# One layer of a hybrid encoder trunk on one core: the value stage's transposed rows by VectorE for the second token half, token sums by token tile and one step later

## The chip, the cores and the metric

The kernel runs on one core of one Trainium2 chip. The core has TensorE (matmuls; PE in the profile, PEld its weight loads), VectorE (DVE), ScalarE (ACT), GpSimd (POOL) and SyncE (SP, whose queue issues nearly all DMAs here). The metric is the device time of one execution in microseconds; the figure compared is the median of several runs.

## The reference, cut to what matters

All inputs and outputs are f32; 2048 tokens of width 1024. The layer is a token mixer, a cross-attention into 256 memory tokens and a SwiGLU feed-forward, each with a norm before and after it:

```
y = concat([ya, yh]) @ w_out;           h = x + rms_norm(y, g_mix_post)
u = rms_norm(h, g_x_pre)
y = cross_attention(u, m, wq, wk, wv, wo);  h = h + rms_norm(y, g_x_post)
u = rms_norm(h, g_ffn_pre)
y = (silu(u @ w_gate) * (u @ w_up)) @ w_down
return h + rms_norm(y, g_ffn_post)
```

The change lies between the second and the third part: where `h` after the cross-attention is formed and `u` of the feed-forward is brought into the layout that the feed-forward's matmuls need.

## The kernel before, in words

f32 accuracy is kept by writing each operand as a high and a low part (`split2`: ScalarE rounds to the high part, VectorE subtracts to get the low part) and taking three products (`products`, lines 1162 to 1164).

The second half of the kernel is a row of jobs, and `phases` runs them: output projection (`mixed_block`), scores (`score_block`), values (`value_block`), the hidden layer for the first and the second half of the tokens (`hidden_blocks`), and the down projection in three pieces. A job is a 1024 x 1024 matrix (or part of one) that stays in SBUF as split tiles, the resident tiles `T`, against which blocks of 256 rows are streamed (`streamed`, tiles `S`). For the hidden layer the resident matrix is u, transposed: 1024 features by 1024 tokens of one half, and the weights are streamed. For the value job 16 token tiles of 128 rows are streamed in eight blocks; block n holds tiles n and n + 1.

A block is multiplied with seven products of quarters in place of eight (`seven`, a Strassen-like form, in the order 1, 5, 6, 3, 7, 2, 4); a product, one step, is 12 matmuls of 128x128 by 128x512. Steps 1, 2 and 3 use a quarter of the resident matrix as it is (`BLOCK`), steps 5, 7, 6 and 4 use sums and differences of quarters. Those are formed ahead by VectorE and kept in DRAM: for the weights by `combined`, for the second token half by `combined` too (`u_s`), for the first token half by `token_sums` (into `u0_s`; the profile leaves digits out of names and shows it as `u_s`). `resident` makes a T tile in two halves: a load into a row tile, then the split into `dst`. There are seven T slots; a slot comes free with its last use in the job before, so the hidden layer's tiles are split while the value job ends.

What a block does after its products is a generator (`after`), and each step moves every open generator on by one `yield`. `value_block.after` does, for its two row tiles: norm scale (line 1657), residual added (1661) and stored, mean squares, norm scale for the feed-forward (1670), then transposition. `transposed` does that with eight TensorE transposes of 128x128 (line 1423) into two PSUM banks and two ScalarE copies (1424); the result is stored into `u_d`. Blocks 4 and 6 (tokens 512 to 1023) then load back the transposed tile that lies 512 tokens earlier and form the sums (1461 to 1465).

`blocked` (line 1431) is another transposition, which the mixed and the score blocks use: VectorE transposes 32x32 blocks in two instructions of 128x512, and `store_blocked` stores the result in four DMAs, each from 32 partitions, such that what lies in DRAM has features on the partition axis.

The order in which each engine gets its instructions is set by a scheduler when the program is built: it goes by the order of the program and by when an instruction is ready in its own model of time. `issue_after` holds an instruction behind another; `behind` does that for a whole block of code, behind the last ScalarE and VectorE instruction of the present step. The splits of T tiles with a lag are put behind so.

Of the kernel before, what the change touches and what calls it, by code (L numbers as in the profile page):

```python
# [11 lines left out]
F32 = mybir.dt.float32  # L12
# [3 lines left out]
ALU = mybir.AluOpType  # L16
AX = mybir.AxisListType

P = 128
T = 2048  # L20
D = 1024
# [3 lines left out]
KT = D // P  # L25
NFF = DFF // P
NB = 2
TB = T // NB
NPB = TB // P
NT = T // P  # L30
# [18 lines left out]
class Layer:  # L49
# [111 lines left out]
    def run(self):  # L161
        tc, nc, I = self.tc, self.nc, self.I
        self._n = 0
        self.last = {}
        kw = dict(reuse_waits="tile")
        self.z_d = tc.dram_tile([DIN, T], F32, name="z_d")

        self.y_d = tc.dram_tile([NT, P, D], F32, name="y_d")
        self.un_d = tc.dram_tile([NPB, 2, P, 512], F32, name="un_d")
        self.h1t_d = tc.dram_tile([NT, 2, P, 512], F32, name="h1t_d")  # L170
        self.pt_d = tc.dram_tile([NT, 2, P, 512], F32, name="pt_d")
        self.h1_d = tc.dram_tile([T, D], F32, name="h1_d")
        self.h2_d = tc.dram_tile([T, D], F32, name="h2_d")
        self.qk_d = tc.dram_tile([D, D], F32, name="qk_d")
        self.vo_d = tc.dram_tile([D, D], F32, name="vo_d")
        self.u_d = tc.dram_tile([KT, P, T], F32, name="u_d")
        self.h_d = tc.dram_tile([NFF, P, T], F32, name="hid_d")
        self.y2_d = tc.dram_tile([T, D], F32, name="y2_d")
        with (
            tc.tile_pool(name="cst", bufs=1) as self.cst,  # L180
            tc.tile_pool(name="sm", bufs=3, **kw) as self.sm,
            tc.tile_pool(name="edge", bufs=1, side="right") as edge,
        ):
            self.consts()
# [281 lines left out]
    def in_first(self):  # L466
# [65 lines left out]
        def fetch():  # L532
            for s in range(2):
                for q in range(2):
# [11 lines left out]
                  for i, p in enumerate(self.ORDER)]  # L546
# [4 lines left out]
        phases = self.phases([(lambda i, j, a, n: raw[i, j][:, a:a + n, :], 4, blocks, None, {})], T)  # L551
# [451 lines left out]

    CHAIN = (5, 7, 6, 4)

    def resident(self, get, nk, key, dst, keep, sums):

        nc = self.nc  # L1010
        halves = [(0, (nk + 1) // 2), ((nk + 1) // 2, nk)]

        def fetched(a, b):
            if key in self.BLOCK:
                return get(*self.BLOCK[key], a, b - a), None
            if sums:
                return get(key, None, a, b - a), None
            if key == 5:
                return get(0, 1, a, b - a), get(0, 0, a, b - a)
            if key == 7:  # L1020
                return get(1, 1, a, b - a), get(0, 1, a, b - a)
            if key == 6:
                return keep[7][len(src)], get(0, 0, a, b - a)
            return get(1, 0, a, b - a), keep[6][len(src)]

        def split(a, b, t, o):
            if o is not None:
                nc.vector.tensor_tensor(t, t, o, ALU.add if key == 6 else ALU.subtract)
            self.split2(t, dst[:, 0, a:b], dst[:, 1, a:b], "A")

        src = []
        for a, b in halves:
            t, o = fetched(a, b)
            src.append(t)
            if key in (6, 7):
                keep[key] = src
            yield lambda a=a, b=b, t=t, o=o: split(a, b, t, o)
# [212 lines left out]
    def phases(self, jobs, first, prologue=None):  # L1250
# [51 lines left out]
        def half(g, tile):  # L1302

            if current[0] is None:
                if not queue:
                    return False
                free = min(slots, key=lambda s: s[1])
                if free[1] > g:
                    return False
                n, p, _ = k = queue.pop(0)  # L1310
                slots.remove(free)
                slots.append((free[0], uses[k][-1], free[2]))
                self._n += 1
# [5 lines left out]
                current[:] = [(k, self.resident(fetch(n, tile), jobs[n][1], p, dst, keep[n], jobs[n][3] is not None)), 0]  # L1319
# [51 lines left out]
        at = 0  # L1371
        self.last = {}
        fresh = False
        for _, nk, bl, _, beside in jobs:
# [83 lines left out]
    def token_sums(self, a, o, n):  # L1458

        nc = self.nc  # L1460
        nc.vector.tensor_tensor(a[:, 4:8], a[:, 4:8], a[:, 0:4], ALU.subtract)
        nc.vector.tensor_tensor(a[:, 0:4], a[:, 0:4], o[:, 0:4], ALU.subtract)
        yield
        nc.vector.tensor_tensor(o[:, 0:4], o[:, 0:4], a[:, 4:8], ALU.add)
        nc.vector.tensor_tensor(o[:, 4:8], o[:, 4:8], o[:, 0:4], ALU.subtract)
        for c, t in enumerate((a[:, 0:4], a[:, 4:8], o[:, 0:4], o[:, 4:8])):
            self.store(self.u0_s[c].rearrange("p (k t) -> p k t", k=4)[:, :, n * P:(n + 1) * P], t)
        yield

    def jobs(self):  # L1470
# [5 lines left out]
                .rearrange("(k p) d -> p k d", p=P))  # L1476

        def ffn_u(b):
            return lambda t, i, j, k0, n: self.load(
                t, self.u_d[4 * i + k0:4 * i + k0 + n, :, b * TB + j * 512:b * TB + (j + 1) * 512]  # L1480
                .rearrange("k p t -> p k t"))
# [7 lines left out]
        def in_turn(*what):  # L1489
# [8 lines left out]
        jobs = [(self.w_out, 4, kinds([self.mixed_block(n) for n in range(0, NT, 2)], 1), self.out_sums, {1: [qk_s[1]]}),  # L1498
                (qk, 4, kinds([self.score_block(n) for n in range(0, NT, 2)]), qk_s[0], {1: [vo_s[1]]}),
                (vo, 4, kinds([self.value_block(n) for n in range(0, NT, 2)]), vo_s[0], {})]  # L1500
        for b in range(NB):
            beside = {2: [in_turn(*(d[1] for d in d_s))]} if b else {4: [u_s[1]]}
            jobs.append((ffn_u(b), 4, kinds([blk for f in range(0, NFF, 2) for blk in self.hidden_blocks(b, f)], 0, "s"),
                         u_s[0] if b else self.u0_s, beside))
        for c, (src, f0, nk) in enumerate(down):
            jobs.append((src, nk, kinds([self.down_block(c, f0, nk, n) for n in range(0, NT, 2)], 0, "s"), d_s[c][0], {}))

        return jobs

# [127 lines left out]
    def value_block(self, n):  # L1637
# [14 lines left out]
        def after():  # L1652
# [16 lines left out]
            for i in range(2):  # L1669
                nc.vector.scalar_tensor_tensor(y[i], y[i], r[:, i:i + 1], self.g_ffn_pre, ALU.mult, ALU.mult)  # L1670
                yield
            for i in range(2):
                u[i] = self.transposed(y[i], y[i])
                self.store_transposed(self.u_d, n + i, u[i])
                if 4 <= n < 8:
                    o[i] = self.row_tile().rearrange("p (k t) -> p k t", k=KT)
                    self.load(o[i], self.u_d[:, :, (n - 4 + i) * P:(n - 3 + i) * P].rearrange("k p t -> p k t"))
                yield
            if o:
                yield  # L1680
                for i in range(2):
                    yield from self.token_sums(u[i], o[i], n - 4 + i)
# [144 lines left out]
```

## Time and profile before

| | us |
|---|---|
| median of 3 runs | 2538.5 |
| the runs | 2534.66, 2538.5, 2538.6 |
| the profiled execution | 2532.53 |
| its span, first to last instruction | 2530.8 |
| TensorE busy in it | 2496.8 |
| VectorE busy in it | 1794.5 |
| ScalarE busy in it | 1262.1 |

The profile is of one execution. Line numbers (L1423) are those of the kernel. A group of instructions is told as engine, operation, output and inputs by the program's names, shape and count, then its busy time and the mean duration of one in ns, and then the idle time of the engine just before it with what ended it. In the timeline a row begins with its start and its length in us. Durations of neighbouring instructions overlap, so the distance between two starts is shorter than a duration. PE idle for a moment is told with the instruction that it waited for in square brackets.

### The profile page before, as it was taken

The numbers are of one execution on the slowest core, as the hardware profiler recorded it, in microseconds if no ns is written. First come the engines' busy times: TensorE is split into PE (matmuls) and PEld (weight loads), VectorE is DVE, ScalarE is ACT, GpSimd is POOL, SyncE is SP. The second block draws the span as 40 slices with busy tenths as digits, with TensorE's granted clock in tenths as the row PEclk, the third lists the DMA queues.
The fourth block names the chain that finished last, engine by engine and source line by source line (L and its number), as shares of the span: only waits on it lengthen the run. The fifth ranks groups of instructions, "written<-read, shape, count | busy, mean of one in ns | idle before, by whom it ended". The sixth has DMA issues, their size and how long they took to land.

```text
span 2530.8 us, 34134 instructions
## 1 busy us (share of the span) xinstructions
PE 2496.8 (99%) x11942; PEld 2087.0 (82%) x11942; DVE 1794.5 (71%) x2863; ACT 1262.1 (50%) x2627; POOL 375.2 (15%) x540
## 2 busy tenths in 40 slices
PE   9999999999999999999999999999999999999998
PEld 8878888888987888878878888888888888888886
DVE  8785488986557889988866655576566557664766
ACT  5453466655565576566753333353333335443543
POOL 4231344321401111112200000000000000000022
PEclk9999999999999999999999999999999999999999
DMA  6455645673887996758944322254354334565776
GB/s 199 152 167 177 176 145 156 199 248 114 276 311 261 299 335 196 251 175 256 346 161 168 135 77 93 80 192 154 129 208 167 117 130 155 182 178 112 228 173 153
DMA packets 305133, 470.07 MB, mean 186 GB/s; under 512 B 21440, under 2 KB 193472, under 8 KB 304960
## 3 DMA queue, kind: packets, MB, share of 16 engines
q1 hardware_dynamic: 298912, 445.86, 52.7%
q0 software_dynamic: 6048, 22.02, 5.1%
q8 instruction: 94, 1.54, 0.3%
q14 instruction: 79, 0.65, 0.1%
HBM read 301.09 MB, written 166.72 MB: 185 GB/s over the span
## 4 chain that ended last, share of the span: by engine, by line
PE 84%; DVE 6%; DMA 4%; ACT 3%; issue 2%; POOL 1%; SPq 0%; DVEq 0%; POOLq 0%; ACTq 0%
PE psm L1164 23%; PE psm L1162 23%; PE psm L1163 22%; PE psg L156 2%; PE psg L158 2%; PE psg L157 2%; DVE T L1002 1%; DVE S L1002 1%; DMA raw<-in_wo_x_dram 1%; ACT junk L1533 1%; SPq L75 0%; DMA row<-h_d 0%; PE pss L156 0%; PE pss L157 0%; PE pss L158 0%
## 5 line engine op out<-in xcount | busy, mean ns | idle before, releaser
L1162 PE MATMUL psm<-T,S 128*128 128x512 f32 x2680 | 1034.3, 391 | 10.3 <-ACT part L1177 5.6
L1163 PE MATMUL psm<-T,S 128*128 128x512 f32 x2680 | 1042.9, 390 | 1.5 <-DVE T L1002 1.4
L1164 PE MATMUL psm<-T,S 128*128 128x512 f32 x2680 | 1029.8, 390 | 3.7 <-DVE S L1002 3.7
L1162 PEld LDWEIGHTS psm<-T,S 128*128 128x128 f32 x2680 | 503.2, 188 | 122.5 <-ACT part L1177 9.9
L1164 PEld LDWEIGHTS psm<-T,S 128*128 128x128 f32 x2680 | 503.4, 188 | 111.1 <-DVE S L1002 6.7
L1163 PEld LDWEIGHTS psm<-T,S 128*128 128x128 f32 x2680 | 503.5, 188 | 107.2 <-DVE T L1002 3.7
L999 ACT ACTIVATE S<-sum 128x512 fp32r<-128x512 f32 (+1 forms) x370 | 224.3, 620 | 375.7 <-PE psm L1164 274.2
L1002 DVE TENSOR_TENSOR S<-sraw,S 128x512 fp32r<-128x512 f32 (+1 forms) x315 | 212.1, 680 | 237.2 <-ACT S L999 234.1
L1177 ACT ACTIVATE part<-psm 128x512 f32<-128x512 f32 x285 | 168.8, 597 | 260.4 <-PE psm L1164 241.9
L1002 DVE TENSOR_TENSOR S<-sum,S 128x512 fp32r<-128x512 f32 (+1 forms) x388 | 258.5, 675 | 45.2 <-ACT S L999 41.2
L999 ACT ACTIVATE S<-sraw 128x512 fp32r<-128x512 f32 (+1 forms) x300 | 184.4, 618 | 109.2 <-PE psm L1164 107.3
L1566 POOL DMA_DIRECT2D y_d<-row x16 | 14.1, 879 | 1077.0 <-DVE row L1748 1026.1
L1002 DVE TENSOR_TENSOR T<-row,T 128x1024 fp32r<-128x1024 f32 (+1 forms) x112 | 131.0, 1186 | 27.7 <-ACT T L999 25.7
L156 PE MATMUL psg<-u,whi 128*128 128x512 f32 x320 | 127.6, 399 | 1.3 <-DVE z L730 1.3
L158 PE MATMUL psg<-u,wlo 128*128 128x512 f32 x320 | 127.4, 399 | 0.0
L157 PE MATMUL psg<-u,whi 128*128 128x512 f32 x320 | 127.4, 398 | 0.0
L1533 ACT ACTIVATE junk<-row 128x512 f32<-128x512 f32 x160 | 99.7, 625 | 43.5 <-DVE row L1555 21.2
L999 ACT ACTIVATE T<-row 128x1024 fp32r<-128x1024 f32 (+1 forms) x112 | 113.4, 1032 | 7.3 <-DMA row<-in_w_down_dram 2.8
L1699 DVE TENSOR_TENSOR row<-psm,part 128x512 f32<-128x512 f32 x66 | 44.1, 688 | 71.3 <-PE psm L1164 71.3
L1002 DVE TENSOR_TENSOR wlo<-raw,whi 128x1024 fp32r<-128x1024 f32 x52 | 64.0, 1232 | 41.4 <-ACT whi L999 30.6
L1748 DVE TENSOR_TENSOR row<-psm,part 128x512 f32<-128x512 f32 x72 | 49.2, 689 | 49.3 <-PE psm L1164 49.1
L831 ACT ACTIVATE S<-S,w_mn 128x256 f32<-128x256 f32 (+1 forms) x128 | 63.1, 496 | 41.4 <-DVE w_mn L827 41.0
(355 smaller groups left out, 3541.3 us busy)
## 6 DMA issues: line engine op xcount, KB each, us to landing
sraw<-in_w_gate_dram SPq DMA_DIRECT2D x44, 512.0 KB, 3.8
sraw<-in_w_up_dram SPq DMA_DIRECT2D x44, 512.0 KB, 3.7
hid_d<-row SPq DMA_DIRECT2D x44, 512.0 KB, 2.7
sraw<-hid_d SPq DMA_DIRECT2D x32, 512.0 KB, 4.4
sraw<-in_w_in_dram SPq DMA_DIRECT2D x48, 256.0 KB, 3.8
z_d<-pair SPq DMA_DIRECT2D x20, 512.0 KB, 3.3
raw<-in_w_in_dram SPq DMA_DIRECT2D x20, 512.0 KB, 4.6
z_d<-z SPq DMA_DIRECT2D x20, 512.0 KB, 3.8
```

The source lines that it names most:

```text
L156: nc.tensor.matmul(ps, ah, bh, start=(i == 0), stop=False)
L157: nc.tensor.matmul(ps, ah, bl, start=False, stop=False)
L158: nc.tensor.matmul(ps, al, bh, start=False, stop=(i == n - 1))
L831: nc.scalar.activation(s[:, r, o:], s[:, r, o:], AF.Exp, bias=mn[:, i:i + 1], scale=-1.0, accum_out=den[:, i:i + 1])
L999: self.nc.scalar.activation(hi, raw, AF.Copy)
L1002: self.nc.vector.tensor_tensor(lo, raw, f32(hi), ALU.subtract)
L1162: nc.tensor.matmul(ps, s[:, 0, k, :], t[:, 0, k, :], start=st, stop=False, **kw)
L1163: nc.tensor.matmul(ps, s[:, 0, k, :], t[:, 1, k, :], start=False, stop=False, **kw)
L1164: nc.tensor.matmul(ps, s[:, 1, k, :], t[:, 0, k, :], start=False, stop=sp, **kw)
L1177: nc.scalar.activation(t, ps, AF.Copy)
L1533: self.nc.scalar.activation(junk, a, AF.Square, scale=float(D) ** -0.5, accum_out=to)
L1748: nc.vector.tensor_tensor(d, a, b, ALU.add)
```

## The change

For token tiles 8 to 15 the normed rows are transposed with `blocked` and stored with `store_blocked` into a new tensor `ut_d`, laid out as [token tile, half of the features, 128, 512]; TensorE's transposes and ScalarE's copies stay for tiles 0 to 7. `u_d` holds the first token half only. Tiles 0 to 3 are stored a second time, as they lie in SBUF, into `uk_d`, and blocks 4 and 6 load them back from there. The token sums come one `yield` later, their VectorE instructions are put `behind` the step's other work, and `u0_s` is laid out by token tile, so that a store has one piece per partition. `resident` gets one more argument, `bytoken`: where it is set, the loaded half tile holds two token tiles with all four feature blocks, and the split writes them into their places through a rearranged view. It is set for all T tiles of the second token half and for the sums' T tiles of the first. The residual's line (1661) is the same before and after.

```
-        self.u_d = tc.dram_tile([KT, P, T], F32, name="u_d")
+        self.u_d = tc.dram_tile([KT, P, TB], F32, name="u_d")
+        self.ut_d = tc.dram_tile([NPB, 2, P, 512], F32, name="ut_d")
+        self.uk_d = tc.dram_tile([4, P, D], F32, name="uk_d")
...
-    def resident(self, get, nk, key, dst, keep, sums):
+    def resident(self, get, nk, key, dst, keep, sums, bytoken):
...
+            if bytoken:
+                v = t.rearrange("p n (a k c) -> p k (n a) c", **bytoken)
+                c = v.shape[-1]
+                self.split2(v, *(dst[:, e, :, a * P:b * P].rearrange("p k (m c) -> p k m c", c=c) for e in range(2)),
+                            "A")
+                return
             self.split2(t, dst[:, 0, a:b], dst[:, 1, a:b], "A")
...
     def token_sums(self, a, o, n):
-        nc.vector.tensor_tensor(a[:, 4:8], a[:, 4:8], a[:, 0:4], ALU.subtract)
-        nc.vector.tensor_tensor(a[:, 0:4], a[:, 0:4], o[:, 0:4], ALU.subtract)
+        with self.behind():
+            nc.vector.tensor_tensor(a[:, 4:8], a[:, 4:8], a[:, 0:4], ALU.subtract)
+            nc.vector.tensor_tensor(a[:, 0:4], a[:, 0:4], o[:, 0:4], ALU.subtract)
         yield
-        nc.vector.tensor_tensor(o[:, 0:4], o[:, 0:4], a[:, 4:8], ALU.add)
-        nc.vector.tensor_tensor(o[:, 4:8], o[:, 4:8], o[:, 0:4], ALU.subtract)
+        with self.behind():
+            nc.vector.tensor_tensor(o[:, 0:4], o[:, 0:4], a[:, 4:8], ALU.add)
+            nc.vector.tensor_tensor(o[:, 4:8], o[:, 4:8], o[:, 0:4], ALU.subtract)
         for c, t in enumerate((a[:, 0:4], a[:, 4:8], o[:, 0:4], o[:, 4:8])):
-            self.store(self.u0_s[c].rearrange("p (k t) -> p k t", k=4)[:, :, n * P:(n + 1) * P], t)
+            self.store(self.u0_s[c, :, n * 512:(n + 1) * 512], t.rearrange("p k t -> p (k t)"))
...
         def ffn_u(b):
+            if b:
+                return lambda t, i, j, n0, n: self.load(
+                    t, self.ut_d[4 * j + n0:4 * j + n0 + n, i].rearrange("n p c -> p n c"))
...
             for i in range(2):
+                if n >= NPB:
+                    self.store_blocked(self.ut_d[n - NPB + i], self.blocked(y[i], self.row_tile()))
+                    yield
+                    continue
                 u[i] = self.transposed(y[i], y[i])
                 self.store_transposed(self.u_d, n + i, u[i])
-                if 4 <= n < 8:
-                    o[i] = self.row_tile().rearrange("p (k t) -> p k t", k=KT)
-                    self.load(o[i], self.u_d[:, :, (n - 4 + i) * P:(n - 3 + i) * P].rearrange("k p t -> p k t"))
+                if n < 4:
+                    self.store(self.uk_d[n + i], y[i])
+                elif n < 8:
+                    o[i] = self.row_tile()
+                    self.load(o[i], self.uk_d[n - 4 + i])
+                    o[i] = o[i].rearrange("p (k t) -> p k t", k=KT)
                 yield
             if o:
+                yield
                 yield
                 for i in range(2):
                     yield from self.token_sums(u[i], o[i], n - 4 + i)
```

More of the change, by code (lines that the diff above doesn't have):

```diff
@@ L550, in in_first @@
                       + [("v", lambda kind: iter([None]), out, after, keep) for _, out, after, keep in plain])
-        phases = self.phases([(lambda i, j, a, n: raw[i, j][:, a:a + n, :], 4, blocks, None, {})], T)
+        phases = self.phases([(lambda i, j, a, n: raw[i, j][:, a:a + n, :], 4, blocks, None, {}, (None, None))], T)
         PE, ACT, DVE, POOL = (getattr(mybir.EngineType, e) for e in ("PE", "Activation", "DVE", "Pool"))
@@ L1318, in half @@
                 left[k] = 2
-                current[:] = [(k, self.resident(fetch(n, tile), jobs[n][1], p, dst, keep[n], jobs[n][3] is not None)), 0]
+                current[:] = [(k, self.resident(fetch(n, tile), jobs[n][1], p, dst, keep[n], jobs[n][3] is not None,
+                                                jobs[n][5][p not in self.BLOCK])), 0]
             k, f = current[0]
@@ L1373, in phases @@
         fresh = False
-        for _, nk, bl, _, beside in jobs:
+        for _, nk, bl, _, beside, _ in jobs:
             for i, (kind, _, out, follow, addend) in enumerate(bl):
@@ L1478, in ffn_u @@
         def ffn_u(b):
+            if b:
+                return lambda t, i, j, n0, n: self.load(
+                    t, self.ut_d[4 * j + n0:4 * j + n0 + n, i].rearrange("n p c -> p n c"))
             return lambda t, i, j, k0, n: self.load(
-                t, self.u_d[4 * i + k0:4 * i + k0 + n, :, b * TB + j * 512:b * TB + (j + 1) * 512]
-                .rearrange("k p t -> p k t"))
+                t, self.u_d[4 * i + k0:4 * i + k0 + n, :, j * 512:(j + 1) * 512].rearrange("k p t -> p k t"))
         def kinds(blocks, n=0, last="p"):
@@ L1497, in jobs @@
         d_s = [sums(f"d_s{c}", src, nk) for c, (src, _, nk) in enumerate(down)]
-        jobs = [(self.w_out, 4, kinds([self.mixed_block(n) for n in range(0, NT, 2)], 1), self.out_sums, {1: [qk_s[1]]}),
-                (qk, 4, kinds([self.score_block(n) for n in range(0, NT, 2)]), qk_s[0], {1: [vo_s[1]]}),
-                (vo, 4, kinds([self.value_block(n) for n in range(0, NT, 2)]), vo_s[0], {})]
+        jobs = [(self.w_out, 4, kinds([self.mixed_block(n) for n in range(0, NT, 2)], 1), self.out_sums, {1: [qk_s[1]]}, (None, None)),
+                (qk, 4, kinds([self.score_block(n) for n in range(0, NT, 2)]), qk_s[0], {1: [vo_s[1]]}, (None, None)),
+                (vo, 4, kinds([self.value_block(n) for n in range(0, NT, 2)]), vo_s[0], {}, (None, None))]
         for b in range(NB):
@@ L1503, in jobs @@
             jobs.append((ffn_u(b), 4, kinds([blk for f in range(0, NFF, 2) for blk in self.hidden_blocks(b, f)], 0, "s"),
-                         u_s[0] if b else self.u0_s, beside))
+                         u_s[0] if b else self.u0_s, beside, (dict(a=4, k=4),) * 2 if b else (None, dict(a=1, k=4))))
         for c, (src, f0, nk) in enumerate(down):
-            jobs.append((src, nk, kinds([self.down_block(c, f0, nk, n) for n in range(0, NT, 2)], 0, "s"), d_s[c][0], {}))
+            jobs.append((src, nk, kinds([self.down_block(c, f0, nk, n) for n in range(0, NT, 2)], 0, "s"), d_s[c][0], {}, (None, None)))
         return jobs
```

## The prediction

> **What bounds the kernel now.** I read the page first (span, busy shares, chain of waits), then the stretches from the score stage to the first hidden blocks, then single instructions there.
>
> ```profile
> span 2530.8 us, 34134 instructions
> PE 2496.8 (99%) x11942; PEld 2087.0 (82%) x11942; DVE 1794.5 (71%) x2863; ACT 1262.1 (50%) x2627; POOL 375.2 (15%) x540
> PE 84%; DVE 6%; DMA 4%; ACT 3%; issue 2%; POOL 1%; SPq 0%; DVEq 0%; POOLq 0%; ACTq 0%
> ...
> 1080.00:1100.00 20.00, 19.80 (x88) 16.04 (x87) 20.00 (x35) 15.33 (x28) 2.22 (x2) 1.00 0.78 255
> 1260.00:1280.00 20.00, 19.32 (x91) 15.18 (x89) 18.55 (x23) 14.04 (x24) 0.09 (x1) 1.00 0.96 332
> 1218.00:1296.00 78.00, 76.45 (x364) 62.29 (x364) 65.85 (x77) 57.58 (x111) 12.37 (x18) 1.00 0.82 284
> ```
>
> The columns of a stretch are its length, then the busy time of PE, PEld, DVE, ACT and POOL, the clock, the DMA share and GB/s. TensorE is the bound: what leaves it shortens the span, unless it then waits longer. VectorE is the second: 20.00 of 20 us at the end of the score stage, 18.55 where the FFN's resident tiles are made. The transposes of the second token half (blocks 8, 10, 12, 14) lie between 1218 and 1296, where VectorE has 78.00 - 65.85 = 12.15 us free.
>
> The profiled execution took 2532.53 us (1.7 around its span). The median of the three runs, 2538.5, stands 6.0 above it, and they spread over 3.9. I work the change out against the profiled one and add it to the median. About 0.2% (5.1 us) is what a measurement of this kernel can tell from no change.
>
> **TensorE's transposes, removed.** Eight row tiles lose eight transposes each.
>
> ```profile
> 1137.86 0.39 PE L1162 MATMUL psm<-T,S 128*128 128x512 f32 x1
> 1138.09 1.03 PE L1423 MATMUL pss<-ident,row 128*128 128x128 f32 x8
> 1138.88 0.47 PE L1163 MATMUL psm<-T,S 128*128 128x512 f32 x1
> 1139.19 0.39 PE L1164 MATMUL psm<-T,S 128*128 128x512 f32 x1
> ...
> 1218.67 0.87 PE pss L1423 x8
> 1289.73 0.87 PE pss L1423 x8
> 1295.17 0.87 PE pss L1423 x8
> ```
>
> Matmuls start 0.23 us apart (1137.86 to 1138.09). The group puts 1138.88 - 1138.09 = 0.79 between two of them and the next start comes 0.31 later, 0.08 over: 0.87, as the chain of waits has it. 8 x 0.87 = **7.0 us off TensorE**. The same eight tiles lose 16 ScalarE copies; ScalarE is half idle, so I count nothing.
>
> **VectorE's transposes, added.** Two per row tile, 16 in all.
>
> ```profile
> L1431 DVE STREAM_TRANSPOSE row<-row 128x512 f32<-128x512 f32 x64 | 40.6, 684 | 0.0
> 1098.63 1.86 DVE row L1431 x3
> ```
>
> The same operation and shape already runs 64 times, three back to back in 1.86: 0.62 each, 16 x 0.62 = 9.9 us. That fits into the 12.15 us free, by 2.2. So by amounts they lie beside TensorE; by order they need not. If none were covered the cost would be 9.9, if all are it is 0; the nearest rows are the two earlier changes of stage, where VectorE makes such transposes (of the mixed and score blocks) while the next stage's resident tiles are split:
>
> ```profile
> PE psm L1164 <- DVE S L1002: 0.6, 1, 0.6
> PE psm L1162 <- ACT part L1177: 0.3, 1, 0.3
> ...
> PE psm L1162 <- ACT S L999: 1.2, 1, 1.2
> PE psm L1164 <- DVE S L1002: 0.9, 1, 0.9
> PE psm L1162 <- ACT part L1177: 0.5, 1, 0.5
> PE psm L1162 <- DVE row L1555: 0.3, 1, 0.3
> ...
> PE psm L1163 <- DVE T L1002: 1.4, 3, 0.8
> ```
>
> These are TensorE's waits from 930 to 960 (mixed to score, 0.9 in sum), 1100 to 1135 (score to value, 2.9) and 1260 to 1300 (value to FFN, 1.4, with TensorE's transposes). With VectorE's I expect the value stage to end like the worse of the first two: 2.9 - 1.4 = **+1.5**; ends -0.5 and +9.9.
>
> The Trainium skill (VectorE: DVE Perf Modes, The three transpose paths and Rules for kernel authors) speaks against the move: VectorE turns only 32x32 blocks, a whole 128x128 one is TensorE's, at 311 against 390 ns (bf16). By these figures the estimate is 64 x 0.39 = 25 us off TensorE and 64 x 0.311 = 20 on VectorE, a net of some -17. The rows of f32 here, 0.87 / 8 = 0.11 and 1.24 / 8 = 0.155, disagree with both, and decide.
>
> **Token sums, one step later and by token tile.** They subtract a first-half tile that is read back from DRAM, and VectorE waits for it:
>
> ```profile
> 1190.29 0.69 DVE L1461 TENSOR_TENSOR row<-row 128x512 f32<-128x512 f32 x1 [2.29 <-DMA u_d<-row]
> 1195.25 0.50 PE L1164 MATMUL psm<-T,S 128*128 128x512 f32 x1 [1.68 <-DVE S L1002]
> ...
> q1 hardware_dynamic: 28413, 33.09, 88.9%
> ...
> u_s<-row SPq DMA_DIRECT2D x16, 256.0 KB, 6.3
> ```
>
> Queued behind that wait are the splits of the streamed tiles, and TensorE misses one for 1.68 us. A step is 12 matmuls x 0.23 = 2.7 us, more than 2.29, and the copy read back (new tensor uk_d) has 4 KB a partition in one piece in place of eight of 512 B. What would be late next is the split itself, which is now put ahead of the sums. **-1.7**; ends -1.7 and 0. The queue rows are from 1180 to 1290, where the DMA engines are 88.9% busy: of 28413 packets the 16 sum stores have 16 x 512, which become 16 x 128, and four read-backs 4 x 1024, which become 4 x 128. That relief I count as nothing, as nothing in the sum rests on a transfer after it. The four added uk_d stores (512 KB each) go out from 1140 to 1165, behind the u_d stores; SP issues them in 0.4 us each and nobody waits until the sums.
>
> **Blocked stores.** Four of 128 KB per row tile for one of 512 KB: 24 more on SP from 1218 to 1296.
>
> ```profile
> L78 SPq DMA_DIRECT2D pt_d<-row x58: 303/464/1135, 964.3 to 1099.7; - x58
> L78 SPq DMA_DIRECT2D u_d<-row x16: 359/377/1459, 1139.8 to 1296.8; - x16
> ```
>
> 32 x 0.46 - 8 x 0.38 = 11.7 us more of SP's time in 78. Behind them in its queue stand the loads of resident and streamed tiles; the score stage issues such stores among such loads, so their effect is in the 2.9 taken above. Not covered, it would be the later T tiles of the last rival. Their pieces stay 512 B.
>
> **Resident tiles by token halves.** A split now writes half the tokens of all four k, so a step's first product waits for both halves, not for one. Half a step is 6 x 0.23 = 1.4 us; it costs that only where a tile comes just in time, and in the FFN's first half only the sums' tiles are so. Three waits for T:
>
> ```profile
> 1271.79 0.50 PE L1163 MATMUL psm<-T,S 128*128 128x512 f32 x1 [0.32 <-DVE T L1002]
> 1278.34 0.50 PE L1163 MATMUL psm<-T,S 128*128 128x512 f32 x1 [0.36 <-DVE T L1002]
> 1281.04 0.50 PE L1163 MATMUL psm<-T,S 128*128 128x512 f32 x1 [0.76 <-DVE T L1002]
> ```
>
> I take half of 1.4, **+0.7** (ends 0 and 2.8, two tiles). The strided split itself costs nothing: the blocked form exists already (u<-pair, 1219 ns against 1219 for T<-row):
>
> ```profile
> L1002 DVE TENSOR_TENSOR T<-row,T 128x1024 fp32r<-128x1024 f32 x105 | 126.4, 1219 | 27.4 <-ACT T L999 25.3 <-DMA row<-u_s 1.7
> L1002 DVE TENSOR_TENSOR u<-pair,u 128x1024 fp32r<-128x1024 f32 x8 | 9.4, 1219 | 0.2 <-ACT u L999 0.2
> ```
>
> The residual is added by VectorE before the change too (the diff does not touch that line): 0.
>
> **Sum.** -7.0 + 1.5 - 1.7 + 0.7 = -6.5: 2526.0 for a run like the profiled one, **2532.0** as a median. This case's own range is 2528 to 2534.
>
> **Rivals.** *The value stage's end is not TensorE's.* For: the chain leaves TensorE at 1225 and runs over others to 1281.
>
> ```profile
> 1232.04 11.43 DMA row<-h_d
> 1247.58 6.49 DMA out_dram<-row
> 1255.37 2.35 DVE T L1002 x2
> ```
>
> Then the groups that count are the three the chain lists (2.6), with the wait of 1.7: -4.3. Added on the chain are the transposes of block 12 (2.5, VectorE is busy without a gap from 1255.37 to 1276) and of block 10 less the 1.93 us it idles just before 1255 (0.6, row below): -1.2, **2537.3**. Against: at the two earlier changes VectorE was as full and TensorE lost no more than 2.9.
>
> ```profile
> 1254.17 1.28 DVE L1670 SCALAR_TENSOR_TENSOR row<-row,q_r,extra 128x1024 f32<-128x1024 f32 x1 [1.93 <-DMA out_dram<-row]
> ```
>
> *Slower: VectorE becomes the bound in front of the T tiles.* If the 12 transposes of blocks 8 to 12 all run ahead of the last T splits and what TensorE saves before is only waited away, the T tiles come 12 x 0.62 = 7.4 later, and both halves are waited for twice, 2.8; off go the last two groups (1.7) and the wait of 1.7: +6.8, **2545.3**. It decides against the change once more than 3.4 us of lateness (six uncovered transposes) reaches those splits. For: nothing holds the new transposes behind the splits, while the splits themselves are held behind their step. Against: 12.15 us of idle time.
>
> *The clock.* After waits of 1.23 and 0.55 us matmuls start 0.43 apart:
>
> ```profile
> 810.92 0.63 PE L1162 MATMUL psm<-T,S 128*128 128x512 f32 x1
> 811.35 0.63 PE L1163 MATMUL psm<-T,S 128*128 128x512 f32 x1
> ...
> 813.91 0.46 PE L1163 MATMUL psm<-T,S 128*128 128x512 f32 x1
> ```
>
> Eight at +0.2: 1.6. After the 1.68 at 1195 it did not happen. If the longer waits near 1280 bring it, the forecast is 2533.6. By the Trainium skill (TensorE: Matmul & The Clock Gate, Part 1) it takes an idle window of about 3.4 us, which none of these waits fills; this trace has it with less.
>
> **How the numbers follow.** Forecast 0.43, value stage's end 0.25, slower 0.22, clock 0.10. The bound for faster is 2533.4: 0.40 of the first, 0.03 of the second and 0.04 of the clock lie below, 0.47. Above 2543.6 lie 0.20 of the third and 0.01 of the second, 0.21. The rest is 0.32. The range goes down to all of 7.0, 1.7 and the 1.4 of T waits gained (2528.4), less half the runs' spread, 2526.5; up into the slower case, 2543.5.
>
> **What would show it.** Right: 64 TensorE transposes and 16 copies left; TensorE's waits from 1180 to 1300 near 3.6 us, none behind L1461; VectorE near 76 of 78 us. Wrong: waits for T of more than 5 us near 1270 to 1290, or SP late with loads behind the blocked stores.

## The result, and the profile after

The median is 2540.47 us (12 runs, 2537.15 to 2544.0) against 2534.75 for the kernel before (12 runs, 2531.76 to 2538.6): a ratio of 1.0022, 95% interval 1.0015 to 1.003. The change made the kernel slower by 5.6 us. The forecast, 2532.0, had the other sign. That the range of 2526.5 to 2543.5 holds the result is luck of its base: it was built on the 2538.5 of three runs, 3.75 above the median of twelve, and its upper end allows 5.0 over that base, less than the 5.6 measured. Below, a difference to before is (ratio - 1) x 2534.75, each ratio taken against runs of the kernel before beside it. The intervals are some 0.001 to each side, about 2.5 us (3.8 for the kernel without transposition, which has four runs), so the difference of two such kernels is known to some 3.5 us.

The page after, the span and the busy times:

```profile
span 2540.5 us, 34029 instructions
...
PE 2493.8 (98%) x11878; PEld 2082.5 (82%) x11878; DVE 1804.4 (71%) x2879; ACT 1252.8 (49%) x2611; POOL 374.0 (15%) x540
```

TensorE does 64 matmuls less (11878 for 11942) and yet the span is 9.7 longer in the profiled runs. The stretches after (length; busy time of PE, PEld, DVE, ACT, POOL; clock; DMA share; GB/s):

```profile
1180.00:1240.00 60.00, 60.00 (x278) 49.91 (x277) 53.84 (x73) 36.82 (x85) 8.86 (x15) 1.00 0.95 313
1240.00:1300.00 60.00, 50.27 (x191) 38.70 (x191) 55.36 (x67) 35.94 (x67) 9.28 (x12) 0.89 0.86 284
...
1218.00:1296.00 78.00, 68.27 (x270) 53.62 (x270) 73.98 (x91) 48.36 (x92) 12.79 (x17) 0.91 0.89 300
```

and the first two of these stretches before:

```profile
1180.00:1240.00 60.00, 58.32 (x277) 48.35 (x276) 51.48 (x68) 37.89 (x88) 10.90 (x16) 1.00 1.02 336
1240.00:1300.00 60.00, 58.45 (x277) 47.19 (x276) 52.38 (x64) 44.27 (x82) 9.40 (x12) 1.00 0.71 247
```

From 1180 to 1240 the change does what it should: TensorE, 58.32 before, is busy without a gap. It is lost from 1240 to 1300, where TensorE falls from 58.45 to 50.27 and from 277 rows (48 of them transposes) to 191, and the granted clock to 0.89. TensorE's waits from 1180 to 1300 after (total us, times, longest), for 3.1 before:

```profile
PE psm L1170 <- ACT part L1185: 5.7, 3, 2.9
PE psm L1170 <- ACT T L1001: 2.7, 3, 1.6
PE psm L1171 <- DVE T L1004: 1.4, 2, 0.8
```

The wait of 1.7 behind the token sums is gone. The largest sum is new: `part` is the copy by which ScalarE empties a PSUM bank (line 1185), and TensorE waits for the bank. ScalarE's timeline after, up to the longest of these waits (the short accumulator reads between the rows are left out):

```profile
1243.20 1.07 ACT L1001 ACTIVATE T<-row 128x1024 fp32r<-128x1024 f32 x1 [2.10 <-DMA row<-u_s]
...
1249.14 0.60 ACT L1570 ACTIVATE row<-psm 128x512 f32<-128x512 f32 x1 [3.05 <-DMA u_s<-row]
...
1255.23 0.62 ACT L1546 ACTIVATE junk<-row 128x512 f32<-128x512 f32 x1
1255.85 0.62 ACT L1546 ACTIVATE junk<-row 128x512 f32<-128x512 f32 x1
1256.46 0.58 ACT L1570 ACTIVATE row<-psm 128x512 f32<-128x512 f32 x1
1256.94 0.62 ACT L1546 ACTIVATE junk<-row 128x512 f32<-128x512 f32 x1
1257.55 0.62 ACT L1546 ACTIVATE junk<-row 128x512 f32<-128x512 f32 x1
1258.16 0.62 ACT L1546 ACTIVATE junk<-row 128x512 f32<-128x512 f32 x1
1258.78 1.05 ACT L1001 ACTIVATE T<-row 128x1024 fp32r<-128x1024 f32 x1
1259.72 0.58 ACT L1185 ACTIVATE part<-psm 128x512 f32<-128x512 f32 x1
```

and TensorE's after, with what it waited for in brackets:

```profile
1257.07 0.39 PE L1172 MATMUL psm<-T,S 128*128 128x512 f32 x1
1260.36 0.49 PE L1170 MATMUL psm<-T,S 128*128 128x512 f32 x1 [2.91 <-ACT part L1185]
1261.88 0.80 PE L1170 MATMUL psm<-T,S 128*128 128x512 f32 x1 [1.03 <-ACT part L1185]
1262.48 0.63 PE L1171 MATMUL psm<-T,S 128*128 128x512 f32 x1
...
1285.01 0.63 PE L1171 MATMUL psm<-T,S 128*128 128x512 f32 x1
1285.44 0.63 PE L1172 MATMUL psm<-T,S 128*128 128x512 f32 x1
1287.81 0.79 PE L1170 MATMUL psm<-T,S 128*128 128x512 f32 x1 [1.74 <-ACT part L1185]
```

TensorE's last matmul ends at 1257.46; ScalarE then still does two mean squares (`junk`) and a split before it comes to the copy. ScalarE was late already: shortly before it had idled 2.10 us for a load from `u_s` and 3.05 us for a store of the token sums into `u_s` (1.91 in the sums' part alone, below). What share of the loss comes from there was not separated.

After the waits matmuls are 0.63 long and start 0.43 apart (1262.48 to 1267.60, and again from 1285.01 to 1291.39): two stretches of 6.8 us at half clock.

```profile
1260.97:1267.79 6.82, 5.91 (x14) 4.70 (x15) 6.82 (x9) 3.60 (x6) 1.88 (x2) 0.50 1.04 380
1284.86:1291.68 6.82, 5.08 (x13) 3.48 (x12) 5.51 (x7) 5.37 (x11) 1.63 (x3) 0.50 0.31 102
```

Fourteen matmuls from 1261.88 on take 2.9 us more than at 0.23 each; eleven from 1285.01 on, without the wait among them, take 2.5 more. With waits of 9.8 - 3.1 = 6.7 more and 7.0 of transposes less, 5.4 for the clock makes +5.1. The traces bear that out: between the same two TensorE instructions (its 5980th, and its 5350th from the end; 1174.31 and 1311.95 after) this stage takes 137.6 us, and 132.9 before, +4.8. The other 4.9 of the 9.7 lie outside it: 1.75 ahead of the stage, in work that the change leaves alone, and 3.2 behind it. Of these, 1.4 come at the start of the second half's hidden layer:

```profile
1702.87 0.74 PE L1170 MATMUL psm<-T,S 128*128 128x512 f32 x2 [1.11 <-ACT T L1001]
```

This wait for a T tile (1.1 or 1.2 us) is in each of the twelve traces of this document in which the second half's T tiles are made by token halves, and in none of the eight others (0.2 at most); from TensorE's 4000th to its 3500th instruction from the end the twelve take 1.4 us longer.

### The profile page after: what moved, and what is told of

Same layout as the page of the kernel before. It is cut to its first block, busy times and chain, and to the rows that moved or that the text cites. A ratio compares the mean times of both kernels' runs of the same rounds, so it can differ in the third digit from the quotient of the medians.

```text
span 2540.5 us, 34029 instructions
## 1 busy us (share of the span) xinstructions
PE 2493.8 (98%) x11878; PEld 2082.5 (82%) x11878; DVE 1804.4 (71%) x2879; ACT 1252.8 (49%) x2611; POOL 374.0 (15%) x540
## 4 chain that ended last, share of the span: by engine, by line
PE 82%; DVE 6%; DMA 4%; ACT 3%; issue 2%; POOL 1%; SPq 1%; DVEq 0%; POOLq 0%; ACTq 0%
PE psm L1170 22%; PE psm L1172 22%; PE psm L1171 22%; PE psg L157 2%; PE psg L156 2%; PE psg L158 2%; DVE T L1004 1%; DVE S L1004 1%; ACT junk L1546 1%; DMA raw<-in_wo_x_dram 1%; DMA u_s<-row 1%; ACT T L1001 1%; DVE sum L1145 0%; DMA ut_d<-row 0%; SPq L75 0%
## 5 line engine op out<-in xcount | busy, mean ns | idle before, releaser
L1729 DVE TENSOR_TENSOR part<-psm,part 128x512 f32<-128x512 f32 x66 | 43.7, 687 | 56.6 <-PE psm L1172 56.6
```

## The experiments

Five theories were tested. L: the token sums, now late and held behind the step's work. V: VectorE's 16 transposes at this place. Q: the 24 more stores on SP's queue. R: the extra row tile that each transposition takes. Within V, when the others had fallen: T, that VectorE's time on the chip costs it; O, that the order costs it which the scheduler wrote once it had to plan with these instructions.

**The two parts alone (L against V).** Token sums alone: rows of the second half are transposed by TensorE again.

```
-                if n >= NPB:
-                    self.store_blocked(self.ut_d[n - NPB + i], self.blocked(y[i], self.row_tile()))
-                    yield
-                    continue
```

> The second token half is transposed by TensorE again, all else as in the changed kernel: the token sums one step later, behind the step, by token tile, read back from uk_d. Theory L (late sums: what is lost is that the sums of token tile 3 end at 1235 in place of 1215, so that their stores and the resident tiles behind them come late and hold ScalarE's queue): as slow as the changed kernel, 2539 to 2543. Theory V (VectorE's transposes fill VectorE ahead of the T splits): near the kernel before or a little under it, 2532 to 2535, with the wait of 1.7 at 1195 gone and under 3 us of TensorE waits near 1280.

Measured 2531.52, ratio 0.9989 (0.998 to 0.9999): -2.8. VectorE's transposes alone, with the token sums as before:

```
-        with self.behind():
-            nc.vector.tensor_tensor(a[:, 4:8], a[:, 4:8], a[:, 0:4], ALU.subtract)
...
+        nc.vector.tensor_tensor(a[:, 4:8], a[:, 4:8], a[:, 0:4], ALU.subtract)
```

> The second token half is transposed by VectorE as in the changed kernel; the token sums stay as before the change (earlier, not held behind the step, by feature block, read back from u_d). Theory L: faster than before by most of the 7.0 us of TensorE transposes, 2528 to 2531. Theory V: as slow as the changed kernel, 2539 to 2542, with TensorE waits of more than 10 us between 1250 and 1295.

Measured 2537.78, 1.0015 (1.0006 to 1.0024): +3.8. Two kernels take one property of the late sums away from the changed kernel: the `with self.behind()` in `token_sums`, and the added `yield`.

> The changed kernel, its token sums no longer held behind the step, still one step later. Theory L with the hold as cause: the sums of tile 3 end near 1217, the T tiles wait for no store, 2529 to 2533. Theory V: no change, 2539 to 2542. If the one step is the cause, also 2539 to 2542, with the sums still near 1230.

> The changed kernel, its token sums at the old step, still held behind it. Theory L with the step as cause: one step is 2.7 us, the last store lands near 1246 in place of 1249, and some 3 us of TensorE waits go, 2536 to 2538. With the hold as cause: 2538 to 2541. Theory V: 2540.

2539.6, 1.0022 (1.0012 to 1.0031), and 2541.61, 1.0027 (1.0015 to 1.0039): neither brings anything back. L falls: the sums by themselves cost nothing, and the loss comes with the transposes.

**The transposes as work that nobody reads.** The sums' part alone, with the 16 instructions added into a tile that is thrown away; TensorE transposes as before.

```
+                if n >= NPB:
+                    self.blocked(y[i], self.row_tile())
                 u[i] = self.transposed(y[i], y[i])
```

> The sums-only kernel (TensorE transposes the second half), and VectorE's 16 transposes made beside them into row tiles that nobody reads and nobody stores: VectorE's load alone, with no TensorE transpose removed and no blocked store. Theory V (VectorE's 9.9 us in front of the T splits is the cost): 2538 to 2545, with TensorE waits of 10 us or more from 1250 to 1295. Theory Q (the 24 more stores on SP hold the loads of the T tiles back): as sums-only, 2531 to 2533.

2539.09, 1.0021 (1.0011 to 1.003): +5.3, that is 8.1 more than without them, and nearly the changed kernel's time although TensorE's transposes are still there. The waits of 10 us that theory V expected were not reached: from 1180 to 1300 they sum to 7.5 here, and to 8.3 with VectorE's transposes alone.

**No transposition at all.** The changed kernel stores the second half's rows as they are, one DMA for a tile:

```
-                    self.store_blocked(self.ut_d[n - NPB + i], self.blocked(y[i], self.row_tile()))
+                    self.store(self.ut_d[n - NPB + i].rearrange("h p s -> p h s"), y[i].rearrange("p (h s) -> p h s", h=2))
```

> The changed kernel without any transposition of the second token half: the normed rows are stored as they are, one DMA a tile (so the second half of the feed-forward works on rows that are not transposed; that part of the computation is left out). Both theories: the 7.0 us of TensorE transposes show on top of the sums-only kernel if TensorE is the bound there, 2524 to 2527. If the end of the value stage is not TensorE's at all, 2529 to 2532, with longer waits near 1270.

2524.88, 0.996 (0.9945 to 0.9975): -10.1. Against the sums' part alone TensorE's 64 transposes are worth 7.3; in one trace of each, between the two TensorE instructions named above, 130.6 us become 123.4, which is 7.2. Its row for 1240 to 1300:

```profile
1240.00:1300.00 60.00, 58.29 (x253) 47.08 (x253) 52.63 (x66) 38.50 (x71) 10.73 (x9) 1.00 0.74 273
```

and its ScalarE timeline at the place that answers to the one shown:

```profile
1251.09 0.64 ACT L1546 ACTIVATE junk<-row 128x512 f32<-128x512 f32 x1
1251.71 1.07 ACT L1001 ACTIVATE T<-row 128x1024 fp32r<-128x1024 f32 x1
1252.66 1.08 ACT L1185 ACTIVATE part<-psm 128x512 f32<-128x512 f32 x2
```

TensorE is busy 58.29 of 60 at full clock, and one mean square stands in front of the split and the copy; after, five mean squares and a row copy do from 1255.23 on.

**Stores, row tiles, and holding them back (Q, R).** First one store of 512 KB for four of 128 KB (VectorE's transposes stay), then VectorE's transposes `behind` the step's work, then transposes inside the row tile, half into half, with one store:

> The changed kernel with VectorE's transposes, but one store of 512 KB in 2 KB pieces a tile in place of four of 128 KB in 512 B pieces (the 32x32 blocks so stay in their wrong places: the second half's layout is left out). Theory V: as the changed kernel, 2538 to 2543. Theory Q: 2526 to 2532.

> The changed kernel, VectorE's transposes held behind the step's other ScalarE and VectorE work, as the sums are. Theory V, if the order within a step is what matters: 2530 to 2535. Theory V, if the amount of VectorE work before the last T split matters: 2538 to 2543, as the T splits still stand after it. Theory Q: 2539 to 2543.

```
+                    for h in range(2):
+                        to, of = (y[i][:, s * 512:(s + 1) * 512] for s in (1 - h, h))
+                        nc.vector.transpose(to.rearrange("p (b k j) -> p b k j", b=4, k=4),
+                                            of.rearrange("p (k b i) -> p b k i", b=4, k=4))
```

> The kernel without transposition of the second half, and 16 transposes by VectorE of the same size within the row tile itself (from one half of it into the other, so what is stored is not the transposed rows: that part is left out): VectorE's time without the extra row tile that a blocked transposition takes from the 12. Theory V (VectorE's time): 2536 to 2541. Theory R (the extra row tiles hold the loads of the T tiles back): 2525 to 2530.

2539.35, 1.0017 (1.0007 to 1.0026); 2538.98, 1.0014 (1.0005 to 1.0024); 2539.92, 1.0024 (1.0012 to 1.0036). The first two are 1.3 and 2.1 below the changed kernel, within the intervals; the third takes no extra tile and no extra store and loses it all. Q and R fall. Holding the transposes back (2538.98) came out as theory V expected if the amount of work counts and not the order within a step; the order of the whole program is taken up below. The third kernel against none at all: 16.2 us for 16 transposes that take 9.9.

**Half of them.** The unread transposes only in blocks 8 and 10, or only in 12 and 14 (`if 8 <= n < 12`, `if n >= 12`):

> Sums-only with VectorE's dead transposes for blocks 8 and 10 alone, eight of 16 (0.62 each, 5.0 us), all well ahead of the T tiles. Theory V with the free time counting (VectorE has some 6 us of idle stretches before 1255): 2531 to 2533.5. If each transposition costs its own time or more wherever it stands: 2535 to 2537.

> Sums-only with VectorE's dead transposes for blocks 12 and 14 alone: four in the stretch where VectorE has no gap, before the last T splits, four after them. Theory V with the free time counting: the first four cost their 2.5 us or more with a slow clock, 2534 to 2538; the last four nothing. If each costs its own time wherever it stands: 2535 to 2537.

2538.34, 1.0015 (1.0006 to 1.0024), and 2537.24, 1.0015 (1.0005 to 1.0024). Either half, 5.0 us of work, costs 6.6 on top of the sums' part, and both together 8.1. A cost by amount would have halved; but the two halves' 13.2 against 8.1 are 5.1 with an uncertainty of some 4.7. In one trace of each the stage is 7.7 and 4.8 longer than in the sums' part, and 8.5 for both, which points the same way. The first half's 2538.34 lies above both expectations.

**Work against order.** The scheduler plans with every instruction, so each kernel so far changed VectorE's work and the orders of all engines together. These four separate them: once all orders are written, only the size of the added transposes is changed, 128x512 to 128x32 or the reverse. A small one still takes 3.0 of the 10.7 us. The group of the added ones, where they are cut, and then where they are grown (total us, mean ns of one):

```profile
L1689 DVE STREAM_TRANSPOSE row<-row 128x32 f32<-128x32 f32 x16 | 3.0, 201 | 0.0
```

```profile
L1689 DVE STREAM_TRANSPOSE row<-row 128x512 f32<-128x512 f32 x16 | 10.7, 693 | 0.0
```

The edit:

```
     with tile.TileContext(nc, schedule_with_timeline_sim=True) as tc:
         Layer(tc, I, out).run()
+    resize(nc, [[D, P], [1, 32]], [[D, P], [1, 32]])
```

> The kernel with the transposes inside the row tile (2539.9 us), its orders kept: the scheduler plans with 16 transposes of 128x512, and once all orders are written each is cut to 128x32. TensorE's order is then that of 2539.9, VectorE's work that of no transposition (2524.9). The transposed rows are left out. If VectorE's time on the chip costs the 15 us (theory T), 2525 to 2527. If the order that the scheduler wrote costs them (theory O), 2537 to 2540. Between the two, both have a share.

> The other way round: the scheduler plans with 16 transposes of 128x32, and once all orders are written each is grown to 128x512. TensorE's order differs in 28 rows of 11142 from that of no transposition (in 115 from that of the kernel with 2539.9 us). The transposed rows are left out. Theory T: 2537 to 2540. Theory O: 2525 to 2528.

> The same pair on the kernel with only the token sums' part and 16 unread transposes (2539.1 us): orders kept, the transposes cut to 128x32 afterwards. All work of the kernel is done. Theory T: near the sums' part alone, 2531.5 to 2533. Theory O: 2537 to 2539.

> The other way round: planned with 128x32, grown to 128x512 once the orders are written. TensorE's order differs in 58 rows from that of the sums' part alone. All work of the kernel is done. Theory T: 2537 to 2539. Theory O: 2531.5 to 2533.

The two corners that were then missing, planned and run with 128x32:

> The fourth corner of the first pair: planned with 16 transposes of 128x32 inside the row tile and run so (3.0 us of VectorE where 128x512 is 10.7). The transposed rows are left out. Known are: planned 512 and run 512 2539.9, planned 512 and run 32 2536.35, planned 32 and run 512 2533.8; no transposition at all 2524.9. If the order written for 32 is as good as that for none, 2525 to 2527, and the 7 to 9 us to 2533.8 are VectorE's work. If that order costs as well, 2530 to 2534, and the work is worth little.

> The fourth corner of the second pair: the sums' part with 16 unread transposes of 128x32, planned and run so. All work of the kernel is done. Known are: 512 and 512 2539.1, planned 512 and run 32 2536.7, planned 32 and run 512 2537.8; none 2531.5. If the order written for 32 is as good as that for none, 2531.5 to 2533; if it costs by itself, 2535 to 2537.5.

Differences to before in us; in brackets the median, and the time of the stage in one trace, between the same two TensorE instructions as above:

| planned with, run with | transposes in the row tile, rows else not transposed | the sums' part and unread transposes |
|---|---|---|
| none, none | -10.1 (2524.88; 123.4) | -2.8 (2531.52; 130.6) |
| 128x32, 128x32 | -7.1 (2527.97; 126.3) | +1.8 (2535.63; 136.4) |
| 128x32, 128x512 | -0.8 (2533.8; 131.2) | +2.8 (2537.77; 138.2) |
| 128x512, 128x32 | +2.3 (2536.35; 134.8) | +3.0 (2536.73; 136.9) |
| 128x512, 128x512 | +6.1 (2539.92; 136.6) | +5.3 (2539.09; 139.1) |

Both theories have a share in the first column: with the order fixed, VectorE's larger work costs 6.3 (order for 128x32) or 3.8 (order for 128x512); with the work fixed, the order costs 9.4 or 6.9. With an uncertainty of some 3.5, only the 3.8 is hardly told from nothing. The traces say the same, with 5.0 or 1.7 for the work and 8.5 or 5.3 for the order. In the second column work costs 1.0 or 2.3 and order 1.2 or 2.5, which the intervals do not tell from nothing, and 4.6 come already with the small transposes, planned and run; there work and order stay unseparated. In both columns, work that is taken away after the orders are written brings back less than a third of the loss (3.8 of 16.2, 2.3 of 8.1; in the traces 1.7 of 13.1, 2.2 of 8.5).

The work's way is seen in the pair with the order for 128x32. TensorE's waits from 1180 to 1300, run with 128x32:

```profile
PE psm L1170 <- ACT part L1185: 1.5, 2, 1.2
PE psm L1170 <- ACT T L1001: 0.8, 2, 0.4
PE psm L1170 <- ACT S L1001: 0.7, 1, 0.7
PE psm L1171 <- DVE T L1004: 0.2, 1, 0.2
```

and run with 128x512:

```profile
PE psm L1170 <- ACT part L1185: 4.6, 1, 4.6
PE psm L1170 <- ACT T L1001: 0.8, 2, 0.4
PE psm L1170 <- ACT S L1001: 0.7, 1, 0.7
PE psm L1171 <- DVE T L1004: 0.2, 1, 0.2
```

The stretch from 1240 to 1300 of the second:

```profile
1240.00:1300.00 60.00, 53.66 (x220) 42.47 (x218) 58.21 (x74) 37.31 (x68) 9.96 (x11) 0.94 0.78 276
```

and two of ScalarE's rows in it:

```profile
1242.87 0.60 ACT L1570 ACTIVATE row<-psm 128x512 f32<-128x512 f32 x1 [2.19 <-DVE row L1689]
...
1250.94 0.64 ACT L1546 ACTIVATE junk<-row 128x512 f32<-128x512 f32 x1 [2.65 <-DVE row L1674]
```

Three waits are the same and one grows from 1.5 to 4.6. It is named after ScalarE's copy, but ScalarE itself was late by VectorE, which is busy 58.21 of 60: it idled 2.19 us for a transposition (L1689) and 2.65 for the residual's sum (1.17 with 128x32), and from 1250.94 to the copy at 1260.00 it has no gap.

The order's way is seen in the other pair. TensorE's three largest waits from 1180 to 1300, planned and run with 128x512:

```profile
PE psm L1170 <- ACT S L1001: 3.5, 2, 2.8
PE psm L1171 <- DVE T L1004: 3.4, 2, 2.7
PE psm L1170 <- ACT part L1185: 1.4, 2, 1.0
```

and planned with 128x512, run with 128x32, with a stretch of the latter:

```profile
PE psm L1170 <- ACT S L1001: 3.5, 2, 2.8
PE psm L1171 <- DVE T L1004: 1.7, 1, 1.7
PE psm L1170 <- ACT part L1185: 1.5, 2, 0.8
...
1240.00:1300.00 60.00, 52.29 (x203) 40.66 (x202) 49.71 (x67) 38.31 (x71) 9.24 (x12) 0.91 0.79 289
```

VectorE is down to 49.71, less than in any kernel above, and TensorE still only 52.29 at a clock of 0.91. The wait for a split of a streamed tile (S) is 3.5 with this order, whether the work is there or not, and 0.7 with the order for 128x32, whether it is there or not. The wait for T halves with the work. ScalarE's copy, the largest wait in the changed kernel (5.7), is small here, although six mean squares stand in front of one copy too (1253.36 to 1257.04; TensorE waits 0.76 for it). So the same loss comes by other waits in other kernels: with the sums at the old step, 6.8 of the waits are for T tiles. The queue of mean squares is what is seen in the changed kernel, and not shown to be the way of the loss in general. In the traces TensorE's own order differs from that without transposition at 162 of 11878 places, all between 1228 and 1318 us (125 in the changed kernel). Which engine's order costs how much was not separated.

**The transposes moved to where VectorE has time.** All work of the change is done: the second half's rows are stored as they are, and a generator beside the first half's hidden blocks loads each tile, turns it behind the step's work and stores it blocked.

```
+    def turned(self):
+        for n in range(NPB):
+            t = self.row_tile()
+            self.load(t, self.ur_d[n])
+            for _ in range(3):
+                yield
+            with self.behind():
+                r = self.blocked(t, self.row_tile())
+            self.store_blocked(self.ut_d[n], r)
+            yield
...
-            beside = {2: [in_turn(*(d[1] for d in d_s))]} if b else {4: [u_s[1]]}
+            beside = {2: [in_turn(*(d[1] for d in d_s))]} if b else {3: [self.turned], 9: [u_s[1]]}
...
-                    self.store_blocked(self.ut_d[n - NPB + i], self.blocked(y[i], self.row_tile()))
+                    self.store(self.ur_d[n - NPB + i], y[i])
```

> The changed kernel, the second half's normed rows stored as they are and taken up again from the fourth block of the hidden layer on, where VectorE is some 55% busy: loaded, transposed by VectorE in blocks held behind the step, stored blocked; the sums of the second half's quarters five blocks later. All work is done. Theory V: near the kernel without transposition, 2525 to 2529, faster than both kernels. If VectorE's transposes cost their time anywhere: 2532 to 2541.

2525.52, 0.9967 (0.9956 to 0.9978): -8.4, faster than both kernels, and 1.7 above no transposition at all, which the intervals do not tell from nothing, with eight loads and eight tiles' stores more. Its stretches:

```profile
1240.00:1300.00 60.00, 58.28 (x254) 47.11 (x253) 54.46 (x68) 40.15 (x74) 10.74 (x9) 1.00 0.71 270
1300.00:1420.00 120.00, 120.00 (x531) 99.34 (x531) 74.06 (x116) 42.20 (x74) 0.00 (x0) 1.00 0.50 160
```

The value stage's end is as without transposes: in the traces the stage takes 123.4 us in both, and TensorE's order is the same up to 1330 us. From 1300 on, with the transposes there (1322.8 to 1399.6) and VectorE busy 74.06 of 120, TensorE has no gap.

## Why the prediction was wrong

- **The step that failed is VectorE's transposes, +1.5.** It set 9.9 us against 12.15 free and took the price from the worse of the two earlier stage changes. From no transposition to the changed kernel it measured -10.1 to +5.6: 15.7 in place of 1.5 (14.2 within the stage, in one trace of each), beyond the upper end of 9.9 too. That end allowed for no more than the work itself. Two things were not in the +1.5: that the scheduler plans with these instructions and writes another order (6.9 to 9.4 in the pair in the row tile, where the work has 3.8 to 6.3), and that half-clock stretches come with TensorE's waits, which stood only among the rivals. VectorE busy 73.98 of 78 came near the 76 forecast, while TensorE's waits are 9.8 for the 3.6 forecast; busy time just did not carry the price. That earlier stages bear the same instruction was a poor measure of this one.
- **TensorE's transposes, -7.0:** right, 7.3 between the sums' part alone and no transposition; the page counts 64 matmuls less, as foretold. But with VectorE's in the same place it is all lost: the unread transposes beside TensorE's, +5.3, and the changed kernel without TensorE's, +5.6, are level.
- **Token sums, -1.7, and T tiles by halves, +0.7:** together -1.0; the sums' part alone measured -2.8 (interval -5.1 to -0.3), and the wait behind them is gone. In that kernel only the sums' T tiles are by halves, and TensorE's waits for T do not appear before 1300. The second half's halves cost 1.4, at the start of that half's hidden layer: the whole half step and not half of it, and at a place that the forecast did not name. The kernel without transposition has this cost too.
- **Blocked stores, 0:** 1.3 against one store, not told from nothing. SyncE's loads wait 4.7 us in all for these stores from 1218 to 1300, but the transposes in the row tile, which have none of them, lose as much.
- **The sum:** -7.3 - 2.8 + 15.7 = +5.6 are steps between the same four kernels, so that they add up is no test. As a change, the forecast of -6.5 missed by 12.1; as a time by 8.5, since its base was too high.
- **The rival on the other side** named the direction, 2545.3, and VectorE as the place, but its way was late T tiles: waits for T are 2.7 + 1.4 = 4.1 after (1.4 before), short of the 5 us that should have shown it, and the largest sum, 5.7, is behind ScalarE's copies. So late T tiles are a part of the loss, not the whole. Its point of decision, six uncovered transposes, was not tried; eight cost 6.6. **The value stage's end is not TensorE's** falls: taking TensorE's transposes away gave their whole time. **The clock**, one stretch of 1.6 at a chance of 0.10, came twice, with 5.4 in all, and with waits that the forecast did not have.

The Trainium skill (VectorE: DVE Perf Modes, Rules for kernel authors), by which a whole 128x128 block belongs to TensorE, gave the sign here, though the estimate from its figures, -17, had the other one. As a rule for the whole kernel the runs do not bear it out: the same blocked transposes, moved to a stage with room, give -8.4 (2525.52) where TensorE's give -2.8 (2531.52).

## What to carry to other kernels

Here free time of a second engine did not cover new work that stands in the queues which feed the bound engine just in time: at a change of stage price it by what is queued behind it, and try it a stage later first. In a program whose order is planned, an edit has two prices, its work and the new order; changing an instruction's size after the orders are written can tell them apart. Where either half of a cost costs nearly as much as the whole, look for an order or a threshold and not for an amount.

## What was not expected of the hardware

Half-clock stretches follow waits of TensorE that add up. In the 3.41 us ahead of the first stretch TensorE is busy 0.49, ahead of the second 1.20 (waits of 1.63 and 0.77); before, around the wait of 1.68 at 1195, it is busy 1.73, and no stretch follows:

```profile
1257.55:1260.96 3.41, 0.49 (x1) 0.19 (x1) 3.40 (x5) 3.41 (x10) 2.97 (x5) 1.00 0.94 220
1281.44:1284.85 3.41, 1.20 (x4) 0.80 (x5) 3.26 (x5) 3.41 (x8) 0.00 (x0) 1.00 0.97 253
...
1192.92:1196.33 3.41, 1.73 (x8) 1.09 (x7) 3.41 (x6) 2.70 (x6) 1.72 (x3) 1.00 1.08 374
```

In each of the twenty traces the stretches, up to the one at the program's end, last 3.41 us or two or three times that, and their starts are whole multiples of 3.413 us apart. On that grid, from 820 us on, all 21 spans of 3.41 us at full clock in which TensorE is idle 1.99 us or more are followed by half clock, and none in which it is idle less than 1.58; in between, 6 of 13 are. So where a wait falls on the grid decides as well as its length. No stretch is in the same place before, in the sums' part alone, with no transposition or with the transposes moved; the longest waits there are 1.7, 1.7, 0.6 and 0.6. By the Trainium skill (TensorE: Matmul & The Clock Gate, Part 1) it takes an idle window of about 3.4 us; no single wait in the changed kernel's stage is that long, so here several shorter ones sufficed. The stretches are not of one execution alone: the mean granted clock is 0.993 to 0.996 in the twelve runs of the changed kernel, and 0.996 to 0.999 in 27 of the kernel before.
